# Dense expert stage in pairs of keys: interleaved activations share the instructions on their gates, and the output follows two keys behind

## The chip, the core and the metric

The kernel runs on one core of one Trainium2 chip. The metric is device microseconds of one launch, from the first to the last instruction with what lies around them; lower is better. Times are medians of several runs, and one more execution of the same program was profiled.

## The reference, cut to what matters

A residual block over 1,024 tokens of width 1,024: a mixer (gated DeltaNet heads beside a linear recurrence), cross-attention into 256 memory tokens, and then a PEER feed-forward layer, which is the part that the change touches:

```python
# per token and head: top 16 of 128 x 128 product keys, softmax gates
idx  = e1 * 128 + e2                       # 8 heads x 16 experts of 16,384
gate = softmax(best)
act  = gelu(einsum('phkd,pd->phk', u_tab[idx], t)) * gate
out  = einsum('phk,phkd->pd', act, v_tab[idx])
x = x + out;  return rmsnorm(x, norm_final_w)
```

Each token takes 128 rows of the table u and 128 rows of the table v (16,384 rows of 1,024 float32 each).

## The kernel before

**Two ways through PEER.** For 512 of the 1,024 tokens (four blocks of 128) the rows are gathered: for each block and each of its 128 experts GpSimd issues an indirect DMA of 128 rows (512 KB) into one of the slots of the tile `rb`, and VectorE (DVE) takes a dot product with it (table u) or adds it, scaled, to the output (table v). That is `step()`, 1,024 steps in all, each one `scalar_tensor_tensor` of 128x1024; up to five gathers are under way, and a slot is fetched again when its step is done. For the other 512 tokens (`TD`) the whole tables are multiplied on TensorE (PE): the **dense stage**, `dense()`. Its gates lie in DRAM (`gd`) as a dense table [16 groups, 128 experts, 512 tokens, 8 keys], mostly zeros, made by `gates()` before. Steps are spread over the kernel: `pe.tick` calls `step()` each time that PE has been given a certain amount of work, in the dense stage so that the steps left end with it.

**The dense stage** runs over 128 keys j, each of 128 experts. `hidden(j)` loads the key's 128 rows of u (transposed beforehand, tile `ur`) and of v (`vr`), 512 KB each, and splits each into a high and a low part of type float32r: `split` casts on ScalarE (`uh`, `vh`) and subtracts on DVE (`ul`, `vl`). 24 products of 512 columns (8 chunks of the width, three products each: high-high, high-low, low-high) make h for 128 experts x 512 tokens in the PSUM bank `dh`. ScalarE applies gelu into `dg`, DVE multiplies by the key's gates, ScalarE casts to `dah`, and DVE subtracts to `dal`. The gates come as tile `G`, [128, 512 tokens, 8 keys], one 2 MB load for each 8 keys, in two buffers; one key's gates are every eighth word of it. A load into a buffer can start when the last multiplication that reads it has been done.

`out(j)` multiplies the activations of key j with v: for three blocks of 128 tokens into six PSUM banks that accumulate over all keys (`po00` to `po21`), 18 products. The fourth block has no bank left for that: at odd j, `last(d)` makes the products of keys j-1 and j into the single bank `po3`, 6 for each half of the columns, and DVE adds the bank to `acc` in SBUF. The second half can start in the bank only when DVE has added the first. So an odd out is 6 + 18 + 6 = 30 products, an even one 18. [...]

**The order** in the program is hidden(0), then for each j: hidden(j+1), out(j). On PE this stands as dh(j+1), out(j), dh(j+2), out(j+1), and so on. The other engines' queues are put in order at compile time by a scheduler that takes what its own model finds ready, the earlier in the program first; so the order in a queue need not be that of the program. Each queue is then run in order. Buffers: `ur`, `vr`, `uh`, `ul` two, `vh`, `vl`, `dah`, `dal` three, `dg` and `G` two.

Every operation of an engine other than PE is issued at line 83 (`f`), every product at line 108 (`matmul`), every indirect DMA at line 1157 (`fetch`); the rows are told apart by the names of the tiles.

Of the kernel before, what the change touches and what calls it, by code (L numbers as in the profile page):

```python
# [8 lines left out]
F = mybir.dt.float32  # L9
BF = mybir.dt.bfloat16  # L10
FR = mybir.dt.float32r
I32 = mybir.dt.int32
U32 = mybir.dt.uint32
AF = mybir.ActivationFunctionType
# [9 lines left out]
TD = 2 * T  # L24
EC = 8
# [24 lines left out]
def block_kernel(ctx: ExitStack, tc: tile.TileContext, a):  # L50
# [76 lines left out]
    act, dve = Engine(nc.scalar, 200.0, 0.72), Engine(nc.vector, 68.0, 1.04)  # L127
# [119 lines left out]
    def c8(t):  # L247
        return t.rearrange("p (c m) -> p c m", c=8)
# [67 lines left out]
    def mm3(out, l, r, start, stop):  # L316
        pe.matmul(out, l[0], r[0], start=start, stop=False)
        pe.matmul(out, l[0], r[1], start=False, stop=False)
        pe.matmul(out, l[1], r[0], start=False, stop=stop)
# [60 lines left out]
    def memory(p, KT, VM):  # L380
        M = []
        buf = p.tile([128, 8, T], F, name="oT", bufs=1)
        for b in range(2):
            t = buf[:, 4 * b:4 * b + 4, :].rearrange("p c t -> p (c t)")
            sp.dma_start(t, a["mem"][b * 128:(b + 1) * 128, :])
            M.append(t)
        mT, _ = yield from norm_T(p, M, 2, wmemc, M, pair=(low(1), lambda: p.tile([128, T], F, name="pqT", bufs=2)))
        for j in range(8):
            ps = yield from proj_T("wk", j, mT, MEM)
            act.copy(KT[:, j, :], ps[:, :MEM])  # L390
        for j in range(8):
            ps = yield from proj("wv", j, mT, 2)
            act.copy(VM[:, :, j * 128:(j + 1) * 128], ps)
# [639 lines left out]
    def u_raw(p, j):  # L1033
        raw = p.tile([128, D], F, name="ur", bufs=2)
        sp.dma_start(raw, a["ut"][j])
        return raw

    def v_raw(p, j):
        raw = p.tile([128, D], F, name="vr", bufs=2)
        sp.dma_start(raw, a["v"][j * 128:(j + 1) * 128, :])  # L1040
        return raw

    def dense(p1, p, ps, hT, raws):
        hhi, hlo = hT
        NT = TD // 128
        res = [[ps.tile([128, 512], F, name=f"po{t}{d}") for d in range(2)] for t in range(NT - 1)]
        acc = p.tile([128, D], F, name="acc", bufs=1)
        row3 = D0 + TD - 128
        sp.dma_start(acc, x2d[row3:row3 + 128, :])

        def split(raw, name, bufs):
            hi = p1.tile([128, D], FR, name=name + "h", bufs=bufs)
            lo = p1.tile([128, D], FR, name=name + "l", bufs=bufs)
            act.copy(hi, raw)
            dve.tensor_sub(lo, raw, hi.bitcast(F))
            return hi, lo

        G = [None]
        A, V = {}, {}

        def hidden(j):
            if j % EC == 0:
                G[0] = p.tile([128, TD, EC], F, name="G", bufs=2)
                sp.dma_start(G[0], gd[j // EC])
            u, v = raws.pop(0) if raws else (u_raw(p1, j), v_raw(p1, j))
            uh, ul = [c8(t) for t in split(u, "u", 2)]
            V[j] = split(v, "v", 3)
            h = ps.tile([128, TD], F, name="dh")
            for c in range(8):
                mm3(h, (uh[:, c, :], ul[:, c, :]), (hhi[:, c, :], hlo[:, c, :]), c == 0, c == 7)  # L1070
            g = p.tile([128, TD], F, name="dg", bufs=2)
            act.activation(g, h, AF.Gelu_apprx_tanh)
            dve.tensor_mul(g, g, G[0][:, :, j % EC])
            ah = p.tile([128, TD], FR, name="dah", bufs=3)
            al = p.tile([128, TD], FR, name="dal", bufs=3)
            act.copy(ah, g)
            dve.tensor_sub(al, g, ah.bitcast(F))
            A[j] = (ah, al)

        xs = []  # L1080

        def add_res(t):
            x = xs[0][:, t, :]
            for d in range(2):
                ds = slice(d * 512, (d + 1) * 512)
                dve.tensor_add(x[:, ds], x[:, ds], res[t][d])
            finish(x, D0 + t * 128, xs[0][:, NT - 1, :])

        def out(j):
            def part(o, i, t, d, start, stop):  # L1090
                ts, ds = slice(t * 128, (t + 1) * 128), slice(d * 512, (d + 1) * 512)
                mm3(o, [x[:, ts] for x in A[i]], [x[:, ds] for x in V[i]], start, stop)

            def last(d):
                o = ps.tile([128, 512], F, name="po3")
                for i in (j - 1, j):
                    part(o, i, NT - 1, d, i < j, i == j)
                ds = slice(d * 512, (d + 1) * 512)
                dve.tensor_add(acc[:, ds], acc[:, ds], o)

            if j == 124:
                xs.append(p.tile([128, TD, EC], F, name="G", bufs=2).rearrange("p (t d) k -> p t (d k)", t=4))
                sp.dma_start(xs[0][:, 0:NT - 1, :],
                             x2d[D0:row3, :].rearrange("(t p) m -> p t m", p=128))
            if j % 2:
                last(0)
            for t in range(NT - 1):
                for d in range(2):
                    part(res[t][d], j, t, d, j == 0, j == 127)
                if j == 127:  # L1110
                    add_res(t)
            if j % 2:
                last(1)
                for i in (j - 1, j):
                    A.pop(i), V.pop(i)

        hidden(0)
        for j in range(128):
            if j + 1 < 128:
                hidden(j + 1)  # L1120
            for _ in range(LATE):
                next(late[0], None)
            out(j)
        finish(acc, row3, xs[0][:, NT - 1, :])
# [80 lines left out]
    def finish(X, row, jk):  # L1205
        ss = small.tile([128, 1], F, name="f_ss")
        act.activation(jk, X, AF.Square, accum_out=ss)
        dve.tensor_scalar(ss, ss, 1.0 / D, EPS, op0=OP.mult, op1=OP.add)
        r = rsqrt(ss, 1, "f_")
        dve.scalar_tensor_tensor(X, X, r, wfin, op0=OP.mult, op1=OP.mult)  # L1210
        sp.dma_start(a["out"][row:row + 128, :], X)
# [74 lines left out]
    def attended():  # L1286
        yield from memory(att, KT, VM)
        first.rank = FIRST
        for t0, nb in UNITS:
            while t0 not in done:  # L1290
                yield None
            yield from attend(att, t0, nb, KT, VM)
        while D0 + TD - T not in begun:
            yield None
        front.close()
        d1 = ctx.enter_context(tc.tile_pool(name="duv", bufs=1))
        dn.append(d1)
        raws.extend((u_raw(d1, j), v_raw(d1, j)) for j in range(2))

    dn, hT, raws, begun = [], [], [], set()  # L1300
    wp = front.enter_context(tc.tile_pool(name="wp", bufs=1))
    att = front.enter_context(tc.tile_pool(name="att", bufs=1))
    KT = att.tile([128, 8, MEM], F, name="KT")
    VM = att.tile([128, 2, D], F, name="VM")
    first = Stream(attended(), 2, SHARE[1])
    together(Stream(mixed(), RANK[1], SHARE[0]), first)
    fps.close()
    with tc.tile_pool(name="dn", bufs=1, side="right") as d2, \
            tc.tile_pool(name="dps", bufs=1, space=bass.MemoryType.PSUM) as dps:
        pe.pace, pe.real = DENSE / (2.0 * (S - TD) - stepped[0]), False  # L1310
        dense(dn[0], d2, dps, hT, raws)
    while step():
        pass

# [63 lines left out]
```

## Time and profile before

| | |
|---|---|
| median of 3 runs | 3226.76 us (3224.28 to 3238.54) |
| the profiled execution | 3238.51 us; span of its instructions 3236.7 us |
| PE busy | 2982.7 us (92%), 16,212 products |
| DVE busy | 2723.6 us (84%), 5,999 instructions |
| ScalarE (ACT) busy | 1281.2 us (40%) |
| GpSimd (POOL) busy | 1454.7 us (45%) |
| granted clock of PE, mean | 0.964 |
| moved by DMA | 941.66 MB, mean 291 GB/s |

Durations are those of the one profiled execution. Products are pipelined: a product's row shows 0.40 us, but in a stretch without gaps the next one starts 0.23 us after it, so the distance between starts is the price of one. An engine's instructions also overlap a little with their successors. "idle before" is the time that an engine stood before an instruction, with what ended it. A share of busy time is a mean over stages with different limits.

### The profile page before, as it was taken

Reading aid. Unit: us, or ns where it says so; the run is one execution under the profiler, and the core shown is the slowest. Engines: PE = TensorE matmul, PEld = TensorE weight load, DVE = VectorE, ACT = ScalarE, POOL = GpSimd, SP = SyncE. Lnnn points to the kernel's source line nnn. Section 1 sums busy time; section 2 is a strip of 40 time slices with the busy share of each in tenths; the row PEclk is TensorE's granted clock in tenths of the full one; section 3 lists DMA queues with packets and bytes.
Section 4 is the critical chain, followed back from the end, with each engine's and each line's share of the span. In section 5 each row is a group of like instructions: output and inputs, shape, how many; then the busy total and the mean of one; then the engine's idle time right before and its main releaser. Section 6 shows DMA issues by size and latency. Waiting matters only on the chain.

```text
span 3236.7 us, 46492 instructions
## 1 busy us (share of the span) xinstructions
PE 2982.7 (92%) x16212; PEld 2554.5 (79%) x16212; DVE 2723.6 (84%) x5999; ACT 1281.2 (40%) x2694; POOL 1454.7 (45%) x1046
## 2 busy tenths in 40 slices
PE   7899899899999889888667999999999999999998
PEld 6889888888898788777566778778877778788786
DVE  7652578888786987999997999888999999899999
ACT  6844264255315531656575322222222232222222
POOL 0000023245232443343423776666666666666673
PEclk9999999999999999998778999999999999999999
DMA  5244769888787778889978899999999989999996
GB/s 172 92 150 144 228 235 323 307 303 307 274 293 252 249 284 303 295 302 302 308 249 289 303 354 326 339 325 342 355 350 339 344 313 360 325 343 353 345 347 211
DMA packets 321547, 941.66 MB, mean 291 GB/s; under 512 B 28912, under 2 KB 108832, under 8 KB 319264
## 3 DMA queue, kind: packets, MB, share of 16 engines
q0 software_dynamic: 148048, 538.04, 46.8%
q1 hardware_dynamic: 107216, 367.08, 31.5%
q10 hardware_dynamic: 66048, 33.56, 3.7%
q8 instruction: 128, 2.10, 0.3%
q14 instruction: 107, 0.88, 0.1%
HBM read 894.53 MB, written 44.04 MB: 290 GB/s over the span
## 4 chain that ended last, share of the span: by engine, by line
PE 49%; DVE 25%; DMA 12%; issue 7%; ACT 5%; POOL 2%; SPq 0%; another core or an unknown queue 0%; DVEq 0%; POOLq 0%; ACTq 0%
PE dh L108 15%; PE po L108 14%; PE pj L108 14%; DVE rb L83 8%; PE gd L108 4%; DMA rb<-in_v,idx 4%; DVE oh L83 3%; DMA gd<-stage 2%; POOL rb L1157 2%; DMA rb<-in_u,idx 2%; PE tp L113 1%; DVE i L83 1%; DMA w<-in_pwq 1%; PE sc L108 1%; DVE dg L83 1%
## 5 line engine op out<-in xcount | busy, mean ns | idle before, releaser
L1157 POOL DMA_INDIRECT rb<-in_u,idx x512 | 701.2, 1369 | 1104.2 <-DVE lxf L83 419.7
L1157 POOL DMA_INDIRECT rb<-in_v,idx x512 | 744.5, 1454 | 638.8 <-DVE rb L83 429.7
L83 DVE SCALAR_TENSOR_TENSOR rb<-rb,ga 128x1024 f32<-128x1024 f32 x512 | 655.8, 1281 | 29.5 <-DMA rb<-in_v,idx 23.9
L83 DVE SCALAR_TENSOR_TENSOR rb<-rb 128x1024 f32<-128x1024 f32 x512 | 611.2, 1218 | 31.4 <-DMA rb<-in_u,idx 31.3
L108 PE MATMUL pj<-hT,w 128*128 128x256 f32 (+1 forms) x2880 | 591.4, 357 | 16.0 <-DMA w<-in_pwq 14.4
L108 PEld LDWEIGHTS pj<-hT,w 128*128 128x128 f32 x2880 | 491.0, 195 | 70.8 <-DMA w<-in_pwq 14.5
L108 PE MATMUL po<-vh,dah 128*128 128x512 f32 x1024 | 408.5, 399 | 27.7 <-DVE acc L83 27.7
L108 PE MATMUL dh<-hT_h,uh 128*128 128x512 f32 x1024 | 409.9, 400 | 7.6 <-ACT dg L83 6.9
L108 PE MATMUL dh<-hT_h,ul 128*128 128x512 f32 x1024 | 408.3, 399 | 2.1 <-DVE ul L83 2.1
L108 PE MATMUL dh<-hT_l,uh 128*128 128x512 f32 x1024 | 408.5, 399 | 0.0
L108 PE MATMUL po<-vl,dah 128*128 128x512 f32 x1024 | 408.1, 399 | 0.0
L108 PE MATMUL po<-vh,dal 128*128 128x512 f32 x1024 | 406.8, 398 | 0.0
L83 ACT CAST uh<-ur 128x1024 fp32r<-128x1024 f32 x128 | 134.7, 1053 | 602.2 <-PE dh L108 399.8
L108 PE MATMUL gd<-ohg,oh 128*128 128x128 f32 x1024 | 182.7, 335 | 83.3 <-ACT ohg L83 66.1
L108 PEld LDWEIGHTS po<-vh,dah 128*128 128x128 f32 x1024 | 193.4, 189 | 80.4 <-DVE acc L83 33.4
L108 PEld LDWEIGHTS gd<-ohg,oh 128*128 128x128 f32 x1024 | 165.9, 234 | 99.7 <-ACT ohg L83 91.8
L108 PEld LDWEIGHTS dh<-hT_h,uh 128*128 128x128 f32 x1024 | 195.2, 191 | 56.2 <-ACT dg L83 7.8
L108 PEld LDWEIGHTS dh<-hT_h,ul 128*128 128x128 f32 x1024 | 194.4, 190 | 50.6 <-DVE ul L83 2.9
L108 PEld LDWEIGHTS dh<-hT_l,uh 128*128 128x128 f32 x1024 | 195.0, 190 | 47.4
L108 PEld LDWEIGHTS po<-vl,dah 128*128 128x128 f32 x1024 | 193.8, 189 | 47.1
L108 PEld LDWEIGHTS po<-vh,dal 128*128 128x128 f32 x1024 | 193.7, 189 | 46.8
L83 ACT CAST dah<-dg 128x512 fp32r<-128x512 f32 x128 | 79.6, 622 | 305.1 <-DVE dg L83 302.4
(341 smaller groups left out, 4806.0 us busy)
## 6 DMA issues: line engine op xcount, KB each, us to landing
ur<-in_ut SPq DMA_DIRECT2D x128, 512.0 KB
vr<-in_v SPq DMA_DIRECT2D x128, 512.0 KB
w<-in_wA SPq DMA_DIRECT2D x80, 512.0 KB
w<-in_pwq SPq DMA_DIRECT2D x80, 512.0 KB
gd<-stage ACTq DMA_DIRECT2D x32, 1024.0 KB
G<-gd SPq DMA_DIRECT2D x16, 2048.0 KB
w<-in_wout SPq DMA_DIRECT2D x40, 512.0 KB
w<-in_wq SPq DMA_DIRECT2D x40, 512.0 KB
```

The costliest lines, as they stand in the source:

```text
L83: r = call(*args, **kw)
L108: self.engine.matmul(out, l, r, **kw)
L113: self.engine.transpose(out, i, ident)
L1157: pool.indirect_dma_start(out=t, out_offset=None, in_=a[ph], in_offset=bass.IndirectOffsetOnAxis(ap=B["idx"][:, k:k + 1], axis=0))
```

## The change

The activations of two keys, an even one and the odd one behind it, are kept interleaved in one tile `dg` of [128, 512, 2]. gelu still runs once for each key, and writes every second word. After the odd key one multiplication takes both keys' gates, which lie side by side in `G`; one cast and one subtraction make `dah` and `dal` for both, of [128, 2, 512], reading `dg` with a step of two words. These tiles have two buffers of the double size instead of three. The split of v is a function of its own, `values(j)`, and the order in the program is hidden(0), values(0), hidden(1), then for each j: values(j+1), hidden(j+2), out(j). The list of raw loads is parted into one for u and one for v.

```diff
-    def dense(p1, p, ps, hT, raws):
+    def dense(p1, p, ps, hT, raws, rawv):
...
-        A, V = {}, {}
+        A, V, g2 = {}, {}, [None]
 
         def hidden(j):
             if j % EC == 0:
                 G[0] = p.tile([128, TD, EC], F, name="G", bufs=2)
                 sp.dma_start(G[0], gd[j // EC])
-            u, v = raws.pop(0) if raws else (u_raw(p1, j), v_raw(p1, j))
+            u = raws.pop(0) if raws else u_raw(p1, j)
             uh, ul = [c8(t) for t in split(u, "u", 2)]
-            V[j] = split(v, "v", 3)
             h = ps.tile([128, TD], F, name="dh")
             for c in range(8):
                 mm3(h, (uh[:, c, :], ul[:, c, :]), (hhi[:, c, :], hlo[:, c, :]), c == 0, c == 7)
-            g = p.tile([128, TD], F, name="dg", bufs=2)
-            act.activation(g, h, AF.Gelu_apprx_tanh)
-            dve.tensor_mul(g, g, G[0][:, :, j % EC])
-            ah = p.tile([128, TD], FR, name="dah", bufs=3)
-            al = p.tile([128, TD], FR, name="dal", bufs=3)
-            act.copy(ah, g)
-            dve.tensor_sub(al, g, ah.bitcast(F))
-            A[j] = (ah, al)
+            if j % 2 == 0:
+                g2[0] = p.tile([128, TD, 2], F, name="dg", bufs=2)
+            g = g2[0]
+            act.activation(g[:, :, j % 2], h, AF.Gelu_apprx_tanh)
+            if j % 2:
+                dve.tensor_mul(g, g, G[0][:, :, j % EC - 1:j % EC + 1])
+                ah = p.tile([128, 2, TD], FR, name="dah", bufs=2)
+                al = p.tile([128, 2, TD], FR, name="dal", bufs=2)
+                g = g.rearrange("p t k -> p k t")
+                act.copy(ah, g)
+                dve.tensor_sub(al, g, ah.bitcast(F))
+                for k in range(2):
+                    A[j - 1 + k] = (ah[:, k, :], al[:, k, :])
+
+        def values(j):
+            V[j] = split(rawv.pop(0) if rawv else v_raw(p1, j), "v", 3)
...
         hidden(0)
+        values(0)
+        hidden(1)
         for j in range(128):
             if j + 1 < 128:
-                hidden(j + 1)
+                values(j + 1)
+            if j + 2 < 128:
+                hidden(j + 2)
             for _ in range(LATE):
                 next(late[0], None)
             out(j)
...
-        raws.extend((u_raw(d1, j), v_raw(d1, j)) for j in range(2))
+        for j in range(2):
+            raws.append(u_raw(d1, j))
+            rawv.append(v_raw(d1, j))
```

## Rows read from the trace of the kernel before

**Rows 1.** The page's first part: busy us, share of the span, count.

```profile
PE 2982.7 (92%) x16212; PEld 2554.5 (79%) x16212; DVE 2723.6 (84%) x5999; ACT 1281.2 (40%) x2694; POOL 1454.7 (45%) x1046
```

**Rows 2.** View by stretches: length, busy us by engine, PEclk, DMA share, GB/s.

```profile
2200.00:2400.00 200.00, 200.00 (x858) 160.79 (x857) 183.84 (x227) 56.61 (x72) 134.17 (x88) 1.00 0.95 351
...
1760.00:3224.00 1464.00, 1433.48 (x6080) 1147.49 (x6079) 1351.18 (x1609) 408.88 (x519) 954.77 (x613) 0.99 0.91 332
```

**Rows 3.** View of waits, 1750 to 3200: us in total, times, longest.

```profile
PE po L108 <- DVE acc L83: 27.7, 11, 5.0
...
DVE ul L83 <- ACT uh L83: 33.1, 23, 2.9
...
DVE rb L83 <- DMA rb<-in_u,idx: 22.2, 9, 6.0
DVE rb L83 <- DMA rb<-in_v,idx: 20.6, 12, 4.8
```

**Rows 4.** View by groups, 1760 to 3224: busy us, mean ns, idle before.

```profile
L83 DVE SCALAR_TENSOR_TENSOR rb<-rb,ga 128x1024 f32<-128x1024 f32 x362 | 464.4, 1283 | 25.0 <-DMA rb<-in_v,idx 20.6
...
L83 DVE SCALAR_TENSOR_TENSOR rb<-rb 128x1024 f32<-128x1024 f32 x256 | 303.5, 1221 | 22.3 <-DMA rb<-in_u,idx 22.2
...
L83 DVE TENSOR_TENSOR dg<-dg,G 128x512 f32<-128x512 f32 x126 | 149.8, 1189 | 1.0 <-ACT dg L83 0.8
...
L83 DVE TENSOR_TENSOR dal<-dg,dah 128x512 fp32r<-128x512 f32 x126 | 86.9, 689 | 1.4
L83 ACT CAST dah<-dg 128x512 fp32r<-128x512 f32 x126 | 78.3, 622 | 304.3 <-DVE dg L83 301.6 <-issue 2.6
L83 ACT ACTIVATE dg<-dh 128x512 f32<-128x512 f32 x126 | 74.3, 589 | 11.0 <-PE dh L108 11.0
```

**Rows 5.** Timeline of DVE in an ordinary pair: start us, us, what, idle before.

```profile
2306.83 1.23 DVE L83 TENSOR_TENSOR ul<-ur,uh 128x1024 fp32r<-128x1024 f32 x1 [1.14 <-ACT uh L83]
2307.97 1.22 DVE L83 TENSOR_TENSOR dg<-dg,G 128x512 f32<-128x512 f32 x1
2309.09 0.71 DVE L83 TENSOR_TENSOR acc<-acc,po 128x512 f32<-128x512 f32 x1
...
2312.94 0.69 DVE L83 TENSOR_TENSOR acc<-acc,po 128x512 f32<-128x512 f32 x1 [2.36 <-PE po L108]
```

**Rows 6.** Timelines of ScalarE and PE in the same pair.

```profile
2305.75 1.05 ACT L83 CAST uh<-ur 128x1024 fp32r<-128x1024 f32 x1 [5.74 <-PE dh L108]
...
2312.24 2.00 ACT L83 CAST vh<-vr 128x1024 fp32r<-128x1024 f32 x2 [2.39 <-PE po L108]
...
2311.34 0.40 PE L108 MATMUL po<-vh,dah 128*128 128x512 f32 x1
```

**Rows 7.** Timelines by engine of the stretch 2017 to 2035.

```profile
2017.57 0.33 SPq L83 DMA_DIRECT2D G<-gd  x1
...
2020.39 1.45 POOL L1157 DMA_INDIRECT rb<-in_u,idx  x1 [0.30 <-issue]
...
2032.04 1.22 DVE L83 SCALAR_TENSOR_TENSOR rb<-rb 128x1024 f32<-128x1024 f32 x1 [6.03 <-DMA rb<-in_u,idx]
...
2034.18 0.68 DVE L83 TENSOR_TENSOR acc<-acc,po 128x512 f32<-128x512 f32 x1
...
2029.56 0.40 PE L108 MATMUL po<-vh,dal 128*128 128x512 f32 x1
2034.92 0.80 PE L108 MATMUL po<-vh,dah 128*128 128x512 f32 x1 [4.96 <-DVE acc L83]
```

**Rows 8.** Chain of waits, first and last piece of eight; loads of G.

```profile
1922.59 11.82 DMA rb<-in_v,idx
...
3033.23 10.59 DMA rb<-in_v,idx
...
L83 SPq DMA_DIRECT2D G<-gd x14: 326/327/327, 1828.7 to 3034.6; - x14
```

**Rows 9.** View by stretches, behind that stop.

```profile
2034.90:2038.00 3.10, 3.08 (x7) 2.48 (x8) 3.10 (x6) 1.14 (x3) 1.34 (x2) 0.50 0.86 300
```

More of the change, by code (lines that the diff above doesn't have):

```diff
@@ L1297, in attended @@
         dn.append(d1)
-        raws.extend((u_raw(d1, j), v_raw(d1, j)) for j in range(2))
-    dn, hT, raws, begun = [], [], [], set()
+        for j in range(2):
+            raws.append(u_raw(d1, j))
+            rawv.append(v_raw(d1, j))
+    dn, hT, raws, rawv, begun = [], [], [], [], set()
     wp = front.enter_context(tc.tile_pool(name="wp", bufs=1))
@@ L1310, in block_kernel @@
         pe.pace, pe.real = DENSE / (2.0 * (S - TD) - stepped[0]), False
-        dense(dn[0], d2, dps, hT, raws)
+        dense(dn[0], d2, dps, hT, raws, rawv)
     while step():
```

## The prediction

> **What bounds the kernel now.** I read the page first, for busy shares. TensorE (PE) is busy 92% of the span and VectorE (DVE) 84% [rows 1]; such averages mix stages, so I cut the span. The dense stage, the only one that the change touches, fills the last 1,490 us, from the first dh product at 1731 to the last po product at 3223. The view by stretches gives its price: between 2200 and 2400 PE starts 858 products in 200.0 us without a gap, 0.2331 us each [rows 2]. From 1760 to 3224 it starts 6,080, worth 6080 x 0.2331 = 1,417 us, in 1,464 us: **47 us are lost**. PE is busy 1433.5 us of them, so 30.5 us are idle and some 16 us are products at a lower rate [rows 2]. Nothing in the change alters the number or size of the products; a dense stage that loses nothing is the floor.
>
> The view of waits names the loss: PE waits 27.7 us, 11 times, up to 5.0, for DVE's addition to acc [rows 3]. That is the single bank po3: its second half of columns may start only when DVE has added the first half to acc. In an ordinary pair of keys the 30 products of an odd out start as dh ends, about 2305.75 [rows 6]; DVE waits 1.14 us for the cast of u, splits u, multiplies by the gate and adds to acc, done at 2309.80 [rows 5]; PE wants the bank at 2311.34 [rows 6]. So DVE may be late by 1.54 + 1.14, say 2.7 us, before PE stands.
>
> Why is it later? The timelines from 2017 to 2035 show one case [rows 7]. The multiplication of the group's eighth key ends, SP issues the 2 MB load of the next gates at 2017.57, a gather issued at 2020.39 lands at 2032.0 (11.6 us), DVE idles 6.0 us for it, acc is added at 2034.18, and PE, ready at about 2029.8, starts at 2034.92. In the chain of waits eight such gathers of 10 to 14 us start between 1922 and 3033, within 5 us of one of the 14 gate loads [rows 8]; DVE waits 42.8 us for gathers in all [rows 3]. [...]
>
> **The change part by part.** Per pair of keys (22.4 us of PE, 96 products):
>
> *Gate multiplication.* Removed: two of 512 columns at 1.189 us [rows 4]. Added: one of 1,024. The old one reads every eighth word of G and costs twice acc's 512 columns (0.71, rows 5); the new one reads two adjacent words, then hops. Bounds: 1.23 us, as the contiguous 1,024-column split of u [rows 5], and 2 x 1.19 = 2.38. I take 1.23: where both words of a hop are used, the hop should be paid at most once, and the row for 512 hops is 1.19.
>
> *Subtraction.* Removed: two of 0.689 [rows 4]. Added: one of 1,024 that reads its first operand every second word. No row shows that step. Bounds: 1.23 (as contiguous) and 2.38 (as the eight-word step). Neither end is clearly nearer; I take the middle, 1.8. [...]
>
> DVE per pair: 2.38 + 1.38 = 3.76 removed, 1.23 + 1.8 = 3.03 added; two instructions fewer also lose their overlap of some 0.1 each with the next one (ul starts 2306.83, lasts 1.23, the next starts 2307.97). Net saving about 0.5 us, between 0 and 1.1. Over 64 pairs 34 us of DVE time (0 to 70), but **DVE does not set the end**: it is busy 1,351 of 1,464 us [rows 2], so this is worth only what it takes off PE's 30 us of stops.
>
> *ScalarE.* gelu stays two of 512 (0.589), now writing every second word; two casts of 0.622 become one of 1,024 that reads every second word [rows 4]: 1.05 to 2.5 us. ScalarE is busy 409 of 1,464 us [rows 2], and what follows has time: after the odd dh PE runs out (7.0 us) and the next dh (5.6) before it needs the new pair. The chain uh, gelu, multiplication, cast, subtraction is 1.05 + 0.6 + 1.23 + 1.05..2.5 + 1.23..2.4 = 5.2 to 7.8 us against 12.6. Cost nothing; without that cover it would be PE's wait on dal.
>
> *The lag.* PE's products are the same. Start: three dh before the first out instead of two; the first pair's work (about 1754 to 1759) lies under the third dh. 0 to 3 us. End: dh(127) comes before out(125), so 5.2 to 7.8 us of chain stand under 7.0 us of products: 0 to 1 us. DMAs: u, v and G are the same in number; u is split one key further ahead, v is not.
>
> *What moves.* This is the larger effect. The pair is multiplied after an odd dh, and now the 30 products with the po3 deadline follow that dh; before, the 18 of an even out did. Call the start of the 30 products t = 0: dh at 7.0, 18 products at 12.6, dh at 16.8, the next 30 at 22.4, deadline for acc at about 5.6, then 28. Before, the eighth key's multiplication ended near t = 16 and the gate load met the deadline 12 us later, with gathers 2.8 + 11.6 = 14.4 us after the load's issue. Now the load is issued at t = 3.6, just ahead of an acc that is already next in line; the late gather lands at t = 18, and the next deadline is t = 28. Besides, DVE's work from 12.6 to 22.4 falls: one split (1.14) and 9.8/22.4 of 618/64 = 9.7 gather steps of about 1.2 [rows 4], 6.2 us of 9.8 instead of 8.0 (there a multiplication and a subtraction fall away).
>
> A lag of 6.0 us at t = 18 recovers 4.4 x 3.6/9.8 = 1.6 by t = 22.4 and has 2.7 us to spare: 1.7 us of stop in place of 5.0. The lags of about 5 us leave 0.5 to 1 each, the ones of 2 to 3 nothing. Taking the 27.7 us of waits for acc [rows 3] to follow gate loads, as in rows 7 and 8, about 5 remain, and stops under 2 us cost little of the slow clock, so 12 of its 16 us go as well.
>
> **Sum**, from the profiled execution: 3238.5 - 22 - 12 + 1 (start and end) = 3205. The profiled execution is 11.8 us above the median of the runs, 3226.76, at the top of their range; nothing but stops should differ between runs, so the median run has about 35 us of them, of which 13 remain: 3226.8 - 22 = 3205 again. **Forecast 3205 us, 0.7% faster.** Own range: 3192 (all 47 us gone) to 3211.
>
> **Rivals.**
>
> *The stops stay (no change).* The gathers are late because the DMA queues are at 91% in this stage [rows 2], not because DVE is slow; a DVE that saves 0.5 us only waits longer for the same gather, and the stop moves to another deadline or to another burst (u and v, 0.5 MB each, come every key). For it: in the case of rows 7 DVE is idle for the 6 us, so less work ahead of it gives nothing. Against it: the load moves away from the deadline. At two thirds or more of the stops: 3226.8 - 0 to 12, about 3221.
>
> *The step of two words costs the eight-word price and the lag recovers more slowly.* DVE saves nothing; the shift of the gate load alone works: a gain of 8 to 14 us, about 3216, within 0.5%.
>
> *ScalarE's queue turns round (slower).* The split of v is now written ahead of the split of a later u. A cast of v waits for the end of the 30 products; if it stands in ScalarE's queue before the cast of u that the next dh needs, PE waits 1.05 to 2.0 (v) + 1.05 (u) + 0.25 = 2.4 to 3.3 us per pair, 150 to 210 us in all, and more with the slow clock. It decides only if the u cast is less than one dh and one out ahead. Against it: the queue follows readiness and not the program, for the cast of u at 2305.75 stands ahead of the two of v at 2312.24 [rows 6], though v was written first. Turned in a tenth of the pairs it would still give 3226.8 - 22 + 6 x 6 = 3241.
>
> **How the numbers follow.** Forecast 0.60; stops stay 0.22; slow step 0.07; queue turned, or another new wait such as PE on dal, 0.11. 0.5%, about what a measurement tells, is 16 us: faster below 3211, slower above 3243. So faster 0.60, same 0.29, slower 0.11. The range takes in the first three cases, with 10 us on the far side of the stops that stay: 3192 to 3231.
>
> **What would show each step.** Right: about 64 multiplications of 1,024 columns near 1.23 us and 64 subtractions between 1.23 and 2.4; PE's waits for acc well under 27.7 us; gate loads issued some 4 us into the 30 products, gathers behind them still late by 9 to 12 us, but no stop behind; PE's clock 1.00 in more stretches; DVE's idle time larger. Wrong: PE's waits for acc as long as before, or new rows of PE waiting for dal, ul or dah; casts of v ahead of casts of u with PE idle behind the 30 products; a multiplication of 2.4 us. The forecast fails most easily if late gathers are followed by other late gathers, so that the lag is still there 10 us on.

## The result, and the profile after

The changed kernel takes 3195.74 us (median of 4 runs, 3194.83 to 3197.32), the one before 3232.65 beside it: a ratio of 0.9881, 95% interval 0.9859 to 0.9904, **1.2% faster**. Timed twice more, each time with other kernels on the same chip, it came to 0.9917 (0.9897 to 0.9936) and 0.9908 (0.9881 to 0.9935). The forecast was 0.7%, 3205 us in a range of 3192 to 3231.

The profiled execution has a span of 3193.2 us against 3236.7. The page's first part, as [rows 1]:

```profile
PE 2960.5 (93%) x16212; PEld 2535.3 (79%) x16212; DVE 2655.3 (83%) x5871; ACT 1278.3 (40%) x2630; POOL 1361.6 (43%) x1046
```

DVE has 128 instructions fewer, two for each of 64 pairs, and ScalarE 64 fewer. The view by stretches, a stretch without a gap and the dense stage from 28 us behind its first product, as [rows 2] (length, busy us by engine, granted clock, DMA share, GB/s):

```profile
2360.00:2560.00 200.00, 200.00 (x858) 160.85 (x858) 180.84 (x159) 56.81 (x63) 116.63 (x88) 1.00 0.93 350
1746.00:3179.00 1433.00, 1422.92 (x6083) 1140.04 (x6081) 1281.22 (x1471) 405.52 (x455) 859.67 (x612) 1.00 0.92 339
```

The rate of products is the same, 0.2331 us. 6,083 of them are worth 1,418 us, so 15 us are lost where it was 47: 10 idle (30.5 before), and 5 in which PE counts as busy beyond the price of its products (16 before). DVE is busy 70 us less, with the same number of gather steps.

The 5 us are not the slow clock: in this profile the granted clock does not fall once in the whole stretch (mean 1.00, where [rows 2] had 0.99). In the profile of before it fell to 0.50 for 3.4 or 6.8 us at six stops for acc, of 1.99 to 4.96 us ([rows 9] is behind the longest: seven products start in its 3.1 us, 0.44 us each); these 31 us cost 15 of the 16. At its stops for acc of up to 1.69 us it did not fall. In each of the two later profiles of the changed kernel it fell at two stops, of 1.95 to 2.36 us, for 3.4 us each time.

The view of waits over the same part, as [rows 3]:

```profile
DVE rb L83 <- DMA rb<-in_u,idx: 56.2, 38, 4.0
DVE ul L83 <- ACT uh L83: 52.1, 36, 3.9
DVE rb L83 <- DMA rb<-in_v,idx: 20.5, 29, 1.5
...
PE po L108 <- DVE acc L83: 8.7, 9, 1.8
```

PE waits 8.7 us for acc, at most 1.8 at a time, instead of 27.7 and 5.0. DVE now waits longer for gathers, 76.7 us against 42.8, and PE hardly feels it. The groups, as [rows 4] (busy us, mean ns, idle before):

```profile
L83 ACT ACTIVATE dg<-dh 128x512 f32<-128x512 f32 x126 | 79.7, 633 | 13.5 <-PE dh L108 13.5
L83 DVE TENSOR_TENSOR dg<-dg,G 128x1024 f32<-128x1024 f32 x63 | 77.3, 1227 | 4.5 <-ACT dg L83 4.5
L83 DVE TENSOR_TENSOR dal<-dg,dah 128x1024 fp32r<-128x1024 f32 x63 | 76.7, 1218 | 4.8 <-ACT dah L83 4.7
L83 ACT CAST dah<-dg 128x1024 fp32r<-128x1024 f32 x63 | 71.3, 1131 | 148.2 <-DVE dg L83 148.2
```

Both new DVE instructions take as long as the contiguous split of 1,024 columns (1.22 us). The pair at a gate load, where [rows 7] showed a stop of 5 us, in the timelines of SP, ScalarE, DVE and POOL (start, us, what, idle before):

```profile
2171.67 0.33 SPq L83 DMA_DIRECT2D G<-gd  x1
...
2168.20 1.05 ACT L83 CAST uh<-ur 128x1024 fp32r<-128x1024 f32 x1 [8.21 <-PE dh L108]
...
2174.74 2.00 ACT L83 CAST vh<-vr 128x1024 fp32r<-128x1024 f32 x2 [1.93 <-PE po L108]
...
2170.43 1.22 DVE L83 TENSOR_TENSOR dg<-dg,G 128x1024 f32<-128x1024 f32 x1
2171.56 0.68 DVE L83 TENSOR_TENSOR acc<-acc,po 128x512 f32<-128x512 f32 x1
...
2184.46 1.23 DVE L83 SCALAR_TENSOR_TENSOR rb<-rb 128x1024 f32<-128x1024 f32 x1 [3.55 <-DMA rb<-in_u,idx]
...
2195.24 0.68 DVE L83 TENSOR_TENSOR acc<-acc,po 128x512 f32<-128x512 f32 x1
...
2173.66 1.68 POOL L1170 DMA_INDIRECT rb<-in_u,idx  x1 [2.33 <-DVE rb L83]
```

The load is issued as the acc of its own pair is being added; the next gathers are late here too (DVE stands 3.55 us at 2184), but the next acc comes at 2195.24, and PE, which wants the bank at about 2196.2, does not stop. Here the cast of u still stands ahead of those of v.

That gathers behind a load of gates are late is seen over the whole stage: by the landings in the trace of the changed kernel, gathers that are issued within 5 us behind a load land after 10.8 us (median; 9.4 to 12.9), those far from a load after 6.8; in late_G (below) after 12.3 and 6.9.

### The profile page after: what moved, and what is told of

Its sections match the earlier page's. It is cut to its first block, busy times and chain, and to the rows that moved or that the text cites. A ratio compares the mean times of both kernels' runs of the same rounds, so it can differ in the third digit from the quotient of the medians.

```text
span 3193.2 us, 46214 instructions
## 1 busy us (share of the span) xinstructions
PE 2960.5 (93%) x16212; PEld 2535.3 (79%) x16212; DVE 2655.3 (83%) x5871; ACT 1278.3 (40%) x2630; POOL 1361.6 (43%) x1046
## 4 chain that ended last, share of the span: by engine, by line
PE 33%; DVE 23%; issue 18%; POOL 10%; DMA 9%; ACT 6%; POOLq 0%; SPq 0%; DVEq 0%; ACTq 0%
PE pj L108 13%; POOL rb L1170 10%; DVE rb L83 8%; PE dh L108 7%; PE po L108 7%; PE gd L108 4%; DVE oh L83 3%; DMA rb<-in_v,idx 2%; DMA gd<-stage 2%; DVE i L83 1%; PE tp L113 1%; DMA w<-in_pwq 1%; ACT ohg L83 1%; DVE s L83 1%; DVE mr L83 1%
## 5 line engine op out<-in xcount | busy, mean ns | idle before, releaser
L1170 POOL DMA_INDIRECT rb<-in_u,idx x512 | 671.8, 1312 | 1113.9 <-DVE rb L83 433.8
L1170 POOL DMA_INDIRECT rb<-in_v,idx x512 | 680.7, 1330 | 678.2 <-DVE rb L83 472.8
L83 DVE TENSOR_TENSOR ul<-ur,uh 128x1024 fp32r<-128x1024 f32 x128 | 155.6, 1222 | 58.7 <-ACT uh L83 58.2
```

The costliest lines, as they stand in the source:

```text
L83: r = call(*args, **kw)
L1170: pool.indirect_dma_start(out=t, out_offset=None, in_=a[ph], in_offset=bass.IndirectOffsetOnAxis(ap=B["idx"][:, k:k + 1], axis=0))
```

## The experiments

Two theories were set against each other. **A:** the gain is the place of the gate load: it used to fall 12 us ahead of the deadline of acc, and now falls 24 us ahead. **B:** the gain is DVE's saved time. All times below are medians; a ratio is to the kernel before, run beside it. "Lag" is the output two keys behind, and "load in front of" tells which products follow the load of gates.

| kernel | lag | load in front of | DVE per pair | time, us | ratio (95%) | PE waits for acc, us |
|---|---|---|---|---|---|---|
| before (two profiles) | no | 18 products | as before | 3228.8 | 1 | 27.7, 21.3 |
| padded (order and work of before) | no | 18 | as before | 3231.6 | 0.9996 (0.9978 to 1.0015) | 26.1 |
| turned | no | 30 | as before | 3223.9 | 0.9981 (0.9961 to 1.0) | 14.4 |
| lag_turned | yes | 18 | as before | 3226.2 | 0.9976 (0.9959 to 0.9993) | 25.4 |
| lag_only | yes | 30 | as before | 3208.1 | 0.9924 (0.9896 to 0.9953) | 12.9 |
| contig_mul | no | 18 | 1.0 less | 3220.1 | 0.9945 (0.9924 to 0.9966) | 16.8 |
| two_muls | yes | 30 | 1.1 more than changed | 3208.8 | 0.9936 (0.9913 to 0.996) | 12.2 |
| late_G | yes | 10 us later | as changed | 3230.4 | 1.0002 (0.9983 to 1.002) | 44.0 |
| changed, first | yes | 30 | 1.1 less | 3195.7 | 0.9881 (0.9859 to 0.9904) | 8.7 |
| changed, again | yes | 30 | 1.1 less | 3206.6 | 0.9917 (0.9897 to 0.9936) | 8.0 |
| changed, a third time | yes | 30 | 1.1 less | 3203.8 | 0.9908 (0.9881 to 0.9935) | 10.6 |
| spread | yes | 30 | 1.1 less | 3198.6 | 0.9886 (0.9867 to 0.9905) | none |

before stood at 3232.7 beside the first run of the changed kernel, at 3234.9 beside lag_turned, contig_mul, spread and its second, at 3231.6 beside late_G, padded and its third, and at 3228.8 beside the rest.

**lag_only: the lag without the pairs.**

```diff
...
+            g = p.tile([128, TD], F, name="dg", bufs=2)
+            act.activation(g, h, AF.Gelu_apprx_tanh)
+            dve.tensor_mul(g, g, G[0][:, :, j % EC])
+            ah = p.tile([128, TD], FR, name="dah", bufs=4)
+            al = p.tile([128, TD], FR, name="dal", bufs=4)
             act.copy(ah, g)
             dve.tensor_sub(al, g, ah.bitcast(F))
...
```

> The lag of two keys and the new order of the splits, but gelu, gate multiplication, cast and subtraction key by key as before (four buffers of dah and dal). DVE's work per pair is that of the kernel before (3.76 us); the loads of the gates are issued in front of the 30 products, as in the changed kernel. Theory A (the gain comes from where the gate load falls against the deadline of acc): PE's waits for acc fall from 27.7 us to 15 or less, and most of the dense stage's gain of 31 us stays, 18 to 28 us; time about 3206. Theory B (the gain is the DVE time saved, 1.3 us a pair): waits and time as in the kernel before, within 8 us.

3208.1 us: without any saving on DVE 0.76% is gained, where the changed kernel gains 0.83 to 1.19%. B alone is out. The waits:

```profile
DVE rb L83 <- DMA rb<-in_u,idx: 14.4, 20, 1.2
DVE rb L83 <- DMA rb<-in_v,idx: 13.8, 12, 4.6
PE po L108 <- DVE acc L83: 12.9, 7, 4.3
```

**turned: the place without the lag.**

```diff
+            k = (j + 1) % 128
-            if j % EC == 0:
+            if j == 0 or (k and k % EC == 0):
                 G[0] = p.tile([128, TD, EC], F, name="G", bufs=2)
-                sp.dma_start(G[0], gd[j // EC])
+                sp.dma_start(G[0], gd[k // EC])
...
-            dve.tensor_mul(g, g, G[0][:, :, j % EC])
+            dve.tensor_mul(g, g, G[0][:, :, k % EC] if k else G0[0])
...
```

> The kernel before, with the keys taken in the order 1, 2, ..., 127, 0: no lag, no pairs, the same DVE work, but the last key of a group of gates is now at an even place, so that its multiplication, and with it the next load of gates, falls in front of the 30 products instead of the 18. Key 0's gates are copied once to a tile of their own (one more DVE instruction of 512 columns). Theory A: as in lag_only, PE's waits for acc 15 us or less, 15 to 28 us faster than before. Theory B: as before, within 8 us. If lag_only gains and this one does not, the gain is the lag's and not the load's place.

3223.9 us, a gain of 5 where A wanted 15 or more: A as it was stated falls. The loads are where they should be, 24 us ahead of the next deadline, and the long stops are gone, but seven of the 14 loads are followed by a stop of 1.2 to 2.7 us at that deadline. New waits stand beside them:

```profile
PE po L108 <- DVE acc L83: 14.4, 10, 2.7
DVE acc L83 <- PE po L108: 9.0, 10, 1.8
PE po L108 <- ACT dah L83: 4.4, 2, 3.0
```

**lag_turned: the lag with the load at its old place.** The edit of turned in lag_only.

> lag_only with the keys taken in the order 1, 2, ..., 127, 0, so that the gate load falls back to its old place, in front of the 18 products; lag, order and DVE work as in lag_only. It fills the fourth cell beside before, turned and lag_only (3228.8, 3223.9, 3208.1). Theory A2 (the lag and the order that comes with it make most of the 20 us; the load's place is worth 5): 3209 to 3216. Theory A (the place, with the lag, makes the 20 us): 3220 to 3229, with stops of 4 us or more behind gate loads.

3226.2 us: a gain of 8 beside before. Of 14 loads seven are followed by a stop of PE for acc, of 1.0 to 5.3 us, 11 to 13 us after the load; in lag_only three of 14 are, at 23 to 24. With the lag the place is worth 0.5%, without it 0.2%; lag and place together give more (0.76%) than the sum of each alone (0.24% and 0.19%). This excess of 0.3% is not clear of the noise: the half-widths of the three intervals together make about 0.4%. The dense stages of the single profiles point the same way: 1468.3 us with both, 1480.0 with the place alone, 1490.8 with the lag alone, and 1482.9 to 1491.8 with neither.

```profile
DVE rb L83 <- DMA rb<-in_v,idx: 26.5, 11, 4.5
PE po L108 <- DVE acc L83: 25.4, 11, 5.3
```

**late_G: the changed kernel with the load 10 us later.**

```diff
+            old = G[0]
             if j % EC == 0:
                 G[0] = p.tile([128, TD, EC], F, name="G", bufs=2)
...
+            if j and j % EC == 0:
+                late_read = p.tile([128, 1], F, name="lr", bufs=1)
+                act.activation(late_read, h[:, 0:1], AF.Identity, bias=old[:, 0, 0:1])
```

> The changed kernel, but the tile of gates is read once more, one word, by ScalarE right behind the gelu of the next group's first key, so that its buffer comes free, and the next gate load is issued, some 10 us later: about 14 us before the deadline of acc instead of 24. DVE's work, pairs and lag stay. If the place of the load against the deadline makes much of the gain, stops of 2 to 4 us behind gate loads come back, PE waits 18 us or more for acc, and the kernel is 6 to 14 us slower than the changed one. If DVE's saved time alone keeps the late gathers covered, the difference is below 4 us.

3230.4 us: the **whole** gain is gone, 27 us where 6 to 14 were expected, with 15 more ScalarE instructions of one column and nothing else added. 13 of the 14 loads are followed by a stop, of 1.5 to 4.8 us, at a deadline 13 to 14 us behind the load. The waits, and one of the stops in the timelines of SP, DVE and PE:

```profile
PE po L108 <- DVE acc L83: 44.0, 16, 4.8
...
2196.38 0.33 SPq L83 DMA_DIRECT2D G<-gd  x1
...
2207.95 1.23 DVE L83 SCALAR_TENSOR_TENSOR rb<-rb 128x1024 f32<-128x1024 f32 x1 [7.41 <-DMA rb<-in_u,idx]
2209.10 0.08 DVE L83 DVE_READ_ACCUMULATOR rb<-rb 128x1 f32 x1
2209.10 2.36 DVE L83 TENSOR_TENSOR ul<-ur,uh 128x1024 fp32r<-128x1024 f32 x2
2211.38 1.22 DVE L83 TENSOR_TENSOR dg<-dg,G 128x1024 f32<-128x1024 f32 x1
2212.51 0.68 DVE L83 TENSOR_TENSOR acc<-acc,po 128x512 f32<-128x512 f32 x1
...
2213.25 0.80 PE L108 MATMUL po<-vh,dah 128*128 128x512 f32 x1 [3.20 <-DVE acc L83]
2213.84 0.63 PE L108 MATMUL po<-vl,dah 128*128 128x512 f32 x1
```

A late gather as at 2184 in the changed kernel, with twice the wait, lands with 4.6 us of DVE work still to do ahead of acc (2207.95 to 2212.51). So the place is necessary. How much of the gain it makes can't be read from this run: late_G keeps the lag and all that DVE saves, which is worth something by contig_mul below, and yet takes as long as before. Its stops are worse than the old ones: PE waits 44.0 us for acc where it was 27.7, and DVE stands up to 7.6 us for a gather where it was 6.0.

**contig_mul: DVE's time alone, in the order of before.**

```diff
-            dve.tensor_mul(g, g, G[0][:, :, j % EC])
+            dve.tensor_mul(g, g, G[0].rearrange("p t k -> p (t k)")[:, j % EC * TD:(j % EC + 1) * TD])
```

> The kernel before, but each gate multiplication reads 512 adjacent words of the tile of gates instead of every eighth word: the gates of other tokens and keys, so the output is not the reference's; loads, waits and order are those of before. It takes 0.69 us in place of 1.19, 1.0 us less DVE work per pair, with no pairs, no lag and the gate load where it was. Theory B (DVE time): a gain near the step from two_muls to the changed kernel, 10 to 16 us, stops of PE for acc 12 to 20 us. Theory A2 (DVE time counts only once order and lag leave it somewhere to go, since the late gathers behind the gate load meet the deadline as before): 0 to 6 us, with stops of 4 to 5 us still there.

3220.1 us, 15 less than before beside it: what B expected, though the stops are still where A has them (eight, up to 3.9 us, seven of them 13 us behind a load). The multiplication:

```profile
L83 DVE TENSOR_TENSOR dg<-dg,G 128x512 f32<-128x512 f32 x126 | 86.6, 687 | 8.1 <-ACT dg L83 7.7
```

So time saved on DVE does shorten the stops, even where the late gather meets the deadline: the instruction that got cheaper stands between the gather and acc in each of them.

**two_muls: the changed kernel with DVE's time given back.**

```diff
-                dve.tensor_mul(g, g, G[0][:, :, j % EC - 1:j % EC + 1])
+                for k in range(2):
+                    dve.tensor_mul(g[:, :, k], g[:, :, k], G[0][:, :, j % EC - 1 + k])
```

> The changed kernel, but the gate multiplication of a pair as two instructions of 512 columns, each reading every eighth word of G and every second of dg, both after the odd key. DVE's work per pair rises by 1.1 to 1.3 us, to nearly that of the kernel before, in the stretch of the 30 products and ahead of acc; places of loads and waits stay. Theory A: waits for acc rise from 8.7 us to 12 to 20, because 1.1 us stand ahead of acc in each pair; 5 to 12 us slower than the changed kernel, still faster than before by 20 or more. Theory B: the larger part of the gain is gone, within 12 us of the kernel before.

```profile
PE po L108 <- DVE acc L83: 12.2, 8, 3.2
...
L83 DVE TENSOR_TENSOR dg<-dg,G 128x512 f32<-128x512 f32 x126 | 151.9, 1205 | 3.1 <-ACT dg L83 3.1
```

3208.8 us, a ratio of 0.9936 where the changed kernel had 0.9881 to 0.9917: 0.2 to 0.55% for 1.1 us a pair, and PE waits 12.2 us for acc instead of 8 to 10.6. The intervals overlap for two of the three runs of the changed kernel, and lag_only (0.9924) is as fast: without DVE's saving the pairs bring nothing that can be told from noise. As A expected; most of the gain stays.

**spread: more room in front of the deadline.** The changed kernel, with the second half of po3 in the next even out:

```diff
-            def last(d):
+            def last(d, j):
...
             if j % 2:
-                last(0)
+                last(0, j)
+            elif j:
+                last(1, j - 1)
+                for i in (j - 2, j - 1):
+                    A.pop(i), V.pop(i)
+            if j % 2 == 0:
+                values(j + 1)
...
-            if j % 2:
-                last(1)
-                for i in (j - 1, j):
-                    A.pop(i), V.pop(i)
+            if j == 127:
+                last(1, j)
...
-            if j + 1 < 128:
+            if j % 2 and j + 1 < 128:
                 values(j + 1)
```

> The changed kernel, with the products of the second half of po3 moved from the odd out to the start of the next even one (behind the dh between them), so that 42 products instead of 18 lie between the two halves and DVE has 9.8 us in place of 4.2 to empty the bank. v of an odd key is split behind them. If the 10 us of remaining stops for acc (with 2 us of slow clock) are set by that deadline, they fall to 3 or less and the time is 3184 to 3190. If the gathers themselves limit DVE by now (77 us of waiting for them), the stops move to vl or dal and the time is within 4 us of the changed kernel, or above it if the split of v is late for the next out.

3198.6 us, 8 us below the changed kernel on the same chip (their runs: 3191.6 to 3204.9, and 3203.4 to 3215.0). The 3184 to 3190 expected was reckoned from the first run of the changed kernel, on another chip; that run's ratio, 0.9881, is no higher than the 0.9886 here, so the 8 us rest on the comparison on one chip. PE does not wait for acc at all, and the dense stage is all but full (view by stretches):

```profile
1751.00:3173.00 1422.00, 1420.16 (x6084) 1141.00 (x6083) 1284.45 (x1468) 397.01 (x453) 850.03 (x613) 1.00 0.92 341
```

6,084 products are worth 1,418 us, so 4 are lost, and the dense stage is 1451.1 us long against 1460.6 to 1465.2 in three profiles of the changed kernel. Beside them on one chip it is **faster than both kernels**, 1.1% below before.

**before_again, padded, after_again, after_third: the front.** The dense stage began 13.7 us earlier in the profile of the changed kernel, with the same queues in front of it.

> The kernel before, unchanged, for a second profile. The dense stage began at 1731.5 in the profile of before and at 1717.8 in that of the changed kernel, though the queues of all engines are the same up to there. If those 13.7 us are chance waits for weights, this profile's stage begins somewhere between 1710 and 1735, and its dense stage again lasts 1480 to 1495 us with 35 us or more of stops. If the changed kernel does shorten the front, this one begins near 1731.

> The changed kernel once more, for the comparison on one chip and a second profile. Time 3193 to 3200. Its dense stage began at 1717.8; those of before at 1731.5 and 1729.6. If the front is chance, this one begins anywhere from 1715 to 1732; if it goes with the kernel, at 1715 to 1721.

The edit of padded, in the kernel before:

```diff
         acc = p.tile([128, D], F, name="acc", bufs=1)
+        pad = p.tile([128, 2 * D], F, name="pad", bufs=1)
+        dve.memset(pad[:, 0:1], 0.0)
```

> The kernel before with 8 KB more in the SBUF pool of the dense stage (as much as the double-size tiles of the changed kernel add; one word of it is set once, nothing else uses it). Up to now the dense stage begins at 1730 to 1733 in the three profiles with the pool and order of before, and at 1718 to 1725 in the seven others, though the queues in front of it are the same. If the size of the pool makes this, it begins at 1717 to 1726 and the kernel is 5 to 10 us faster; if chance does, the time is that of before within 5 us.

> The changed kernel beside late_G on one chip, 3194 to 3208; a third profile of its stops: 8 to 12 us of waits for acc, dense stage 1460 to 1463 us long.

padded began its dense stage at 1719.0 and took 3231.6 us, 0.9996 of before (0.9978 to 1.0015); before_again began at 1729.6, the changed kernel at 1725.0 and 1728.6 in its later profiles, late_G at 1717.8. So the size of the pool does not shorten the kernel, and the early start in one profile says nothing about the change. The second run of the changed kernel missed its 3193 to 3200 (3206.6). The dense stage's own length wanders less: 1491.8, 1482.9 and (padded) 1489.2 us before, 1460.6, 1461.7 and 1465.2 changed (first dh to last po product, from the timelines).

## Why the prediction was right, and where its sizes were off

**What bounds the kernel.** Right: the products' rate is the floor, and what changed in the dense stage is the time lost on it, 47 to 15 us.

**Gate multiplication.** 1.23 us taken, 1.227 measured.

**Subtraction.** 1.8 taken, the middle of the two bounds; 1.218 measured: the lower bound. Net of overlap the saving on DVE is 1.1 us a pair, the upper bound of 0 to 1.1; 64 x 1.1 = 70 us, which is what the view by stretches shows.

**ScalarE.** Within its bounds: the cast 1.131 us, gelu 0.633 instead of 0.589.

**DVE's time.** The prediction gave it no price of its own. contig_mul prices it at 15 us for 1.0 us a pair in the order of before; two_muls at 6 to 18 for 1.1 in the new one, most of that within the noise. This term was missing from the forecast. It may hold more than DVE's own time: the issue of a gather on GpSimd takes 1.41 us on average in the dense stage of the changed kernel and 1.44 in contig_mul, but 1.56 before, 1.54 in lag_only and 1.57 in two_muls, so in these five it is shorter where DVE's work is. No run parts the two.

**What moves.** The mechanism was right, shown by late_G: with the load 10 us later the gain is gone. The distances were right as well: 12 us before, 24.6 after (2171.67 to about 2196.2). The margin of 2.7 us, taken from an ordinary pair, was too wide: in [rows 7] 6.03 us of waiting for the gather made a stop of 4.96, which leaves 1.1. After the change the margin at such a deadline is narrow too: at 2195.92, with 3.55 us of waiting behind it, acc is done only 0.3 us before PE wants the bank. But the working took the lag and the place as one, and in turned the place alone brings 5 us, at the edge of noise. Why the place pays more with the lag was not shown by a run of its own, and stays open. What the timelines tell: in lag_only 7.0 gather steps of a pair stand between the second addition to acc and the next pair's first, and 2.8 behind that first one, in turned 7.4 and 2.5; and in turned DVE stands 9.0 us for PE in front of the second addition, in lag_only not at all. Both would leave DVE less time to work off a late gather ahead of the deadline. But the place of the steps alone is not it: the changed kernel has 7.8 and 2.0, further that way than turned, and waits only 8.0 to 10.6 us for acc, and lag_turned, with the lag, has 7.5 and 2.2, nearly as before (7.4 and 2.3). The order of the gather steps in DVE's queue is set by the scheduler.

**The stops that remain.** About 5 us of waits for acc expected, 8.7, 8.0 and 10.6 measured. Of the 16 us of products at a lower rate, 15 of them at the granted clock of 0.50, 4 were to stay; none did in the first profile and 3.4 in each of the two others. That stops under 2 us would cost little of it was the author's estimate: up to 1.80 us (first profile) they did not lower the clock, at 1.95 us (a later one) the clock fell for 3.4 us. The 5 us were to stand behind loads of gates; of the nine stops left in the first profile only one does, of 1.8 us. So the argument held there with room to spare, and the other stops come from elsewhere. **Start and end:** +1 expected; the 28.5 us behind the first product lose 13.6 us instead of 13.3, the tail behind the last product is 1.3 longer.

**The sum.** From the profiled execution -22 and -12 were forecast for the dense stage; it became 31 us shorter in that profile, 18 to 31 over two of before and three of the changed kernel. In that profile these two terms held. The median moved 37, 28 and 28 us where 22 were forecast. The scaling to the median run was too careful: it took nothing but stops to differ between runs, while the front differs by up to 15 us in 13 profiles and can carry part of that spread. The agreement is partly the range's: 3192 to 3231 also held the cases of stops that stay and of a slow step.

**The rivals.** Stops that stay: no, though DVE does wait longer for the gathers, as that rival said. A step at the eight-word price: no, 1.218 us. ScalarE's queue turned: no; u is cast at 2168.20 and v at 2174.74, in the order of before, and all waits of PE for `ul` in the changed stage come to 0.7 us.

## What to carry to other kernels

Here a load of 2 MB did its harm some ten microseconds after its issue, in the gathers of 512 KB issued just behind it (10.8 us to land instead of 6.8). Where an engine that keeps the order of its queue (in [rows 7] DVE stood 6.03 us for a gather, with the addition to acc, whose products had run by 2030, behind it) must meet a deadline for TensorE, look at the distance from each large issue to the next such deadline, and not only at the engine's load: 10 us of it undid the whole gain (late_G). And where stops have one deadline behind them, look whether the deadline can be moved: spread took away the stops that a better place and cheaper work had left.

## What the runs showed of the hardware

VectorE read 1,024 float32 in steps of two words in 1.218 us, as fast as adjacent ones (1.22 in the split of u), and multiplied by pairs of words eight apart in 1.227 (both in the changed kernel); single words eight apart cost 1.189 for 512 (before) where adjacent ones cost 0.687 (contig_mul), and 1.205 when the other operand and the output stepped by two words as well (two_muls). ScalarE paid 0.04 us on 0.59 for writing every second word (0.633 in the changed kernel, 0.589 before).
